# A Mamba-2 mixer inside a two-layer decoder trunk: grouping the small TensorE products of the scan

## The chip, the cores and the metric

The kernel runs on one core of a Trainium2 chip. Time is device time in microseconds; the kernel before took 1373.68 us, the median of three runs (1373.65 to 1373.69). One more execution was taken with the hardware profiler. A core has five engines with a queue each: TensorE (PE in the profile; its weight loads are PEld), VectorE (DVE), ScalarE (ACT), GpSimd (POOL) and SyncE (SP, which here only issues DMAs). Each engine takes its instructions in the order of its queue, and engines wait for each other by semaphores.

## The reference

The reference is a trunk of two layers on x of shape (1, 512, 1024), all float32: a Mamba-2 mixer, a convolutional FFN, shared keys and values, differential attention and a second FFN. The change lies in the mixer alone, whose core is this:

```python
def ssd_chunked(xdt, a, bm, cm):
    ...
    a_cs = jnp.cumsum(ac, axis=-1)
    decay_in = jnp.exp(segsum(ac))
    cb = jnp.einsum('bclgn,bcsgn->bcgls', cc, bc)
    y_diag = jnp.einsum('bcgls,bgrcls,bcsgrp->bclgrp', cb, decay_in, xc)
    decay_states = jnp.exp(a_cs[..., -1:] - a_cs)
    states = jnp.einsum('bclgn,bgrcl,bclgrp->bcgrpn', bc, decay_states, xc)
    ...
    y_off = jnp.einsum('bclgn,bcgrpn,bgrcl->bclgrp', cc, states_in, jnp.exp(a_cs))
    return (y_diag + y_off).reshape(b, s, h, p)

def mamba2_mixer(x, ln_g, in_w, conv_w, conv_b, dt_bias, a_log, d_skip, norm_g, out_w):
    zxbcdt = rms_norm(x, ln_g) @ in_w
    ...
    xbc = jax.nn.silu(causal_dwconv(xbc, conv_w, conv_b))
    ...
    y = ssd_chunked(xs32 * dt[..., None], a, bm.astype(jnp.float32), cm.astype(jnp.float32))
    y = y + xs32 * d_skip.astype(jnp.float32)[:, None]
    y = y.reshape(b, s, D_INNER) * jax.nn.silu(z.astype(jnp.float32))
    y = rms_norm(y.reshape(b, s, SSM_GROUPS, D_INNER // SSM_GROUPS), ...)
    return y @ out_w
```

There are 4 groups of 8 heads of 64 columns, 4 chunks of 128 tokens, and 128 states. A chunk's output has a part from the chunk itself (C B^T, times the decays, times x) and a part from the state that the chunks before it left.

## The kernel before, in words

**Projections.** Activations lie transposed: features on the 128 partitions, 512 tokens along the free dimension. A column block of 128 features of the input projection is 24 TensorE products of 128 x 512: for each of 8 row blocks, `mm3` multiplies high weights with high activations (L190), high with low (L191) and low with high (L192). The high and low parts are fp32r numbers, split from float32: the weights' high part by ScalarE (L141), the low part by VectorE (L145). `chunk` makes these splits two blocks ahead. Raw weights come by DMA on SP's queue into three buffers.

**A group.** The loop over g (0 to 3) fetches the decays of its four chunks (POOL's queue: `m`, L609, 512 KB each, and `er`, L614), then projects and convolves B (`bT`), C (`cT`) and four x blocks (`xs`) in `conv_block`. Then comes the scan, woven with the four z blocks. After it VectorE multiplies xs by the activated z (L761, here called gating), ScalarE squares it (L763, `gsq`), POOL and VectorE sum the squares (L768, `gacc`), TensorE transposes the sum (L441, `tr_g`), VectorE takes the inverse root, and TensorE spreads it over the tokens (L451, `al_g`). Group 0's norm stands in the stream of group 1's projections; the other groups have the output projection of the group before in between.

**A chunk of the scan.** `tokens` transposes x (four transposes, L639, `xs` in PSUM), multiplies by dt (`xd`, L641) and by the decay to the chunk's end (`xe`, L644), and transposes B (L646, `bt`), which ScalarE copies (L648). `masked` computes C B^T (L630, `cb`) and multiplies it into the decays `m` (L631), on which `decays` has run POOL's causal mask (L619) and eight ScalarE exponentials (L624) before. `states` computes the part from the state before (L656, `yo`; times `er`, L658) and the new state (L661, `st`; copied by ScalarE for chunk 0, L664, updated by VectorE for others, L666 and L667). `outputs` computes the chunk's own part (L676, `y`) and adds it to x (L680, L683). Transposes are one pass each; the float32 products are two.

**What sets the order.** The source traces instructions, and a list scheduler of the framework sets each engine's order by their dependences and its own estimates. Three things steer it: the order in which the source traces them; `pin`, which keeps an instruction in the traced order; and `tc.issue_after(i)`, which puts what is traced inside it behind instruction i on that instruction's engine. `weave(main, fill, num, den)` traces num steps of `fill` for every den of `main`. PSUM has eight banks of 128 x 512 float32: four for the wide products (`mm_bank`) and four for all else (`aux_bank`).

Of the kernel before, what the change touches and what calls it, by code (L numbers as in the profile page):

```python
# [2 lines left out]

# [1 line left out]

# [4 lines left out]
F32 = mybir.dt.float32  # L10
# [8 lines left out]
P = 128  # L19
T = 512  # L20
D = 1024
KB = D // P
# [17 lines left out]
def trunk_kernel(ctx: ExitStack, tc, x, ssm_ln_g, ssm_in_w, ssm_conv_w, ssm_conv_b, ssm_dt_bias,  # L40
# [19 lines left out]
    def aux_bank(name):  # L60
        return pp.tile([P, T], F32, tag="aux", name=name)
# [127 lines left out]
    def mm3(ps, wh, wl, xh, xl, start, stop):  # L189
        pe.matmul(ps, wh, xh, start=start, stop=False)  # L190
        pe.matmul(ps, wh, xl, start=False, stop=False)  # L191
        pe.matmul(ps, wl, xh, start=False, stop=stop)  # L192


    ones = cp.tile([P, P], F32, name="ones")
# [307 lines left out]
    with tc.tile_pool(name="ssm_y", bufs=1) as yp, tc.tile_pool(name="ssm", bufs=1) as sp:  # L503
        def in_block(key):
            wh, wl = chunk(key)
            if key in ("in32", "in36"):
                return ps_b0 if key == "in32" else ps_b1
            ps = mm_bank("ps_" + key)
            for k in range(KB):
                mm3(ps, wh[:, k, :], wl[:, k, :], xgh[k], xgl[k], k == 0, k == KB - 1)  # L510
            return ps

        def conv_block(j, key, dst):
            ps = in_block(key)
# [78 lines left out]
        class Chunk:  # L593


            def __init__(self, g, c, bT, cT, xs, prev):
                self.g, self.c, self.bT, self.cT, self.xs, self.prev = g, c, bT, cT, xs, prev
                self.hh = slice(c * NH + g * HPG, c * NH + (g + 1) * HPG)
                self.cs = slice(c * P, (c + 1) * P)
                self.tag = "%d_%d" % (g, c)  # L600

            def per_head(self, cols):
                return cols[:, self.hh].unsqueeze(2).to_broadcast([P, HPG, 64])
# [21 lines left out]

            def masked(self):

                cs = self.cs
                ps = aux_bank("cb" + self.tag)
                pe.matmul(ps[:, :P], self.bT[:, cs], self.cT[:, cs], start=True, stop=True)  # L630
                dve.tensor_tensor(out=self.m, in0=self.m, in1=ps[:, :P].unsqueeze(1).to_broadcast([P, HPG, P]),  # L631
                                  op=ALU.mult)

            def tokens(self):

                tag, cs = self.tag, self.cs
                ps = aux_bank("xs" + tag)
                for b in range(4):
                    pe.transpose(ps[:, b * P:(b + 1) * P], self.xs[:, b, cs], ident)  # L639
                self.xd = sp.tile([P, HPG, 64], F32, tag="xd", name="xd" + tag, bufs=2)  # L640
                dve.tensor_tensor(out=self.xd, in0=byh(ps), in1=self.per_head(dt), op=ALU.mult)  # L641
                if self.c < NT - 1:
                    self.xe = sp.tile([P, HPG, 64], F32, tag="xe", name="xe" + tag, bufs=2)
                    dve.tensor_tensor(out=self.xe, in0=self.xd, in1=self.per_head(dl), op=ALU.mult)  # L644
                    ps = aux_bank("bt" + tag)
                    pe.transpose(ps[:, :P], self.bT[:, cs], ident)  # L646
                    self.bt = sp.tile([P, P], F32, tag="bt", name="bt" + tag, bufs=2)
                    act.activation(self.bt, ps[:, :P], AF.Copy)  # L648

            def states(self):  # L650
# [43 lines left out]
                    add_to_stream(m, ps, 16, norm)  # L694
                    yield

        def z_blocks(g, zs):
            for b in range(4):
                ps = in_block("in%d" % (4 * g + b))
                z = sp.tile([P, T], F32, tag="z", name="z%d_%d" % (g, b), bufs=4)  # L700
                dve.tensor_tensor(out=z, in0=ps, in1=rr[0], op=ALU.mult)
                act.activation(z, z, AF.Silu)
                zs.append(z)
                yield
# [36 lines left out]
        for g in range(NG):  # L741
            bT = sp.tile([P, T], F32, tag="bT", name="bT%d" % g, bufs=2)
            cT = sp.tile([P, T], F32, tag="cT", name="cT%d" % g, bufs=2)
            xs_ = sp.tile([P, 4, T], F32, tag="xs", name="xs%d" % g, bufs=2)
            cs = chunks(g, bT, cT, xs_)
            for c in cs:
                c.fetch()
            conv_block(16 + g, "in%d" % (32 + g), bT)
            conv_block(20 + g, "in%d" % (36 + g), cT)
            if g == 0:  # L750
                params_a()
            xs = [xs_[:, b, :] for b in range(4)]
            for b in range(4):
                if b >= 2:
                    cs[b - 2].decays()
                conv_block(4 * g + b, "in%d" % (16 + 4 * g + b), xs[b])
            zs = []
            weave(scan(cs), z_blocks(g, zs), 2, 3)
            acc = None
            for b in range(4):  # L760
                dve.tensor_tensor(out=xs[b], in0=xs[b], in1=zs[b], op=ALU.mult)  # L761
                sq = sp.tile([P, T], F32, tag="gsq", name="gsq%d_%d" % (g, b), bufs=2)
                act.activation(sq, xs[b], AF.Square)  # L763
                if b == 0:
                    acc = sq
                else:
                    a2 = sp.tile([P, T], F32, tag="gacc", name="gacc%d_%d" % (g, b), bufs=2)
                    (pool if b == 1 else dve).tensor_tensor(out=a2, in0=acc, in1=sq, op=ALU.add)  # L768
                    acc = a2
            if g == 0:  # L770
                params_b()
                prev = normed(g, xs, acc)
            elif g < NG - 1:
                run(out_proj(g - 1, *prev, None))
                prev = normed(g, xs, acc)
            else:
                op = out_proj(g - 1, *prev, None)
                for _ in range(3):
                    next(op)
                prev = normed(g, xs, acc)  # L780
                run(op)
# [322 lines left out]
```

## Time and profile before

| What | Value |
|---|---|
| median of 3 runs | 1373.68 us (1373.65 to 1373.69) |
| the profiled execution, own time | 1374.65 us |
| its span (first to last instruction) | 1373.0 us |
| PE busy | 1357.5 us, 99% |
| DVE busy | 917.2 us, 67% |
| ACT busy | 666.0 us, 49% |
| granted TensorE clock | 0.999 |

All times of the trace count from the span's start. A row of the timeline gives start and length in us, engine, source line, operation, output tile <- inputs, sizes and a count; in square brackets the engine's idle time before it and who ended it. Ends of matmuls are modelled, and matmuls overlap, so the distance from one start to the next tells more than a length. A row of the view of waits gives the waiter, whom it waited for, the sum in us, how often, and the longest.

### The profile page before, as it was taken

How to read it: one execution, taken by the hardware profiler on the slowest of the kernel's cores; microseconds unless marked ns; L12 is line 12 of the kernel's file. 1: busy time of each engine (PE TensorE's matmuls, PEld its weight loads, DVE VectorE, ACT ScalarE, POOL GpSimd, SP SyncE). 2: the span in 40 equal slices, each digit the busy share in tenths (PEclk: the TensorE clock that was granted, in tenths of full speed). 3: DMA queues.
4: the chain of work that ended last, by engine and by line, in shares of the span. 5: the costliest groups of instructions: out<-in, count | busy, mean ns of one | idle time of the engine just before them, and what ended most of it. 6: DMA issues, size and time to landing. Idle time of an engine off the chain costs nothing.

```text
span 1373.0 us, 16922 instructions
## 1 busy us (share of the span) xinstructions
PE 1357.5 (99%) x6421; PEld 1097.7 (80%) x6421; DVE 917.2 (67%) x1527; ACT 666.0 (49%) x1100; POOL 94.1 (7%) x121
## 2 busy tenths in 40 slices
PE   9999999999999999999999999999999999999998
PEld 7877887887878888888888877776778888888886
DVE  5989788688877774367755456757787773367741
ACT  5696745552444442244434457758554442244431
POOL 4230301100110000000002000000110000000000
PEclk9999999999999999999999999999999999999999
DMA  7542433432233323333323322221223333333231
GB/s 200 153 151 81 146 105 106 136 89 70 92 92 104 96 92 101 99 93 96 96 87 108 116 77 77 63 81 47 61 87 104 92 96 104 93 93 106 85 104 58
DMA packets 187618, 135.07 MB, mean 98 GB/s; under 512 B 6540, under 2 KB 176976, under 8 KB 187536
## 3 DMA queue, kind: packets, MB, share of 16 engines
q1 hardware_dynamic: 180736, 120.84, 29.2%
q0 software_dynamic: 4496, 12.05, 2.8%
q10 hardware_dynamic: 2304, 1.10, 0.3%
q8 instruction: 50, 0.82, 0.2%
q14 instruction: 32, 0.26, 0.1%
HBM read 131.72 MB, written 2.25 MB: 98 GB/s over the span
## 4 chain that ended last, share of the span: by engine, by line
PE 87%; DVE 7%; ACT 4%; issue 1%; DMA 0%; POOL 0%; POOLq 0%; SPq 0%; ACTq 0%
PE ps_d L192 6%; PE ps_d L190 6%; PE ps_d L191 6%; PE ps_u L190 6%; PE ps_u L192 6%; PE ps_u L191 6%; PE ps_g L191 6%; PE ps_g L192 6%; PE ps_g L190 6%; PE ps_in L191 4%; PE ps_in L190 4%; PE ps_in L192 4%; PE ps_o L191 2%; PE ps_o L192 2%; PE ps_o L190 2%
## 5 line engine op out<-in xcount | busy, mean ns | idle before, releaser
L191 PE MATMUL ps_g<-xgl,wh_g 128*128 128x512 f32 x352 | 137.3, 390 | 1.6 <-DVE xgl L409 1.6
L190 PE MATMUL ps_d<-hh,wh_d 128*128 128x512 f32 x352 | 137.6, 391 | 0.0
L190 PE MATMUL ps_u<-xgh,wh_u 128*128 128x512 f32 x352 | 137.4, 390 | 0.0
L192 PE MATMUL ps_d<-hh,wl_d 128*128 128x512 f32 x352 | 137.4, 390 | 0.0
L190 PE MATMUL ps_g<-xgh,wh_g 128*128 128x512 f32 x352 | 137.2, 390 | 0.0
L191 PE MATMUL ps_d<-hl,wh_d 128*128 128x512 f32 x352 | 137.1, 390 | 0.0
L192 PE MATMUL ps_u<-xgh,wl_u 128*128 128x512 f32 x352 | 137.1, 390 | 0.0
L191 PE MATMUL ps_u<-xgl,wh_u 128*128 128x512 f32 x352 | 137.1, 389 | 0.0
L192 PE MATMUL ps_g<-xgh,wl_g 128*128 128x512 f32 x352 | 137.1, 389 | 0.0
L190 PE MATMUL ps_in<-xgh,wh_in 128*128 128x512 f32 x304 | 121.0, 398 | 0.0
L191 PE MATMUL ps_in<-xgl,wh_in 128*128 128x512 f32 x304 | 120.9, 398 | 0.0
L192 PE MATMUL ps_in<-xgh,wl_in 128*128 128x512 f32 x304 | 119.7, 394 | 0.0
L145 DVE TENSOR_TENSOR wl_d<-wr_d,wh_d 128x1024 fp32r<-128x1024 f32 (+1 forms) x48 | 54.5, 1135 | 91.8 <-ACT wh_d L141 91.6
L141 ACT ACTIVATE wh_d<-wr_d 128x1024 fp32r<-128x1024 f32 (+1 forms) x48 | 47.5, 990 | 129.2 <-PE ps_d L191 115.3
L818 ACT ACTIVATE hh<-vg 128x512 fp32r<-128x512 f32 x44 | 27.8, 632 | 114.9 <-DVE vg L817 114.9
L801 DVE TENSOR_TENSOR uu<-ps_u,nr_f 128x512 f32<-128x512 f32 x44 | 30.4, 692 | 77.6 <-PE ps_u L192 77.5
L191 PEld LDWEIGHTS ps_g<-xgl,wh_g 128*128 128x128 f32 x352 | 66.1, 188 | 15.9 <-DVE xgl L409 2.3
L190 PEld LDWEIGHTS ps_g<-xgh,wh_g 128*128 128x128 f32 x352 | 66.1, 188 | 14.0 <-ACT xgh L408 0.5
L192 PEld LDWEIGHTS ps_u<-xgh,wl_u 128*128 128x128 f32 x352 | 66.1, 188 | 13.8
L192 PEld LDWEIGHTS ps_g<-xgh,wl_g 128*128 128x128 f32 x352 | 66.1, 188 | 13.7
L192 PEld LDWEIGHTS ps_d<-hh,wl_d 128*128 128x128 f32 x352 | 66.1, 188 | 13.7
L191 PEld LDWEIGHTS ps_d<-hl,wh_d 128*128 128x128 f32 x352 | 66.1, 188 | 13.6
(340 smaller groups left out, 2980.4 us busy)
## 6 DMA issues: line engine op xcount, KB each, us to landing
wr_g<-in_ffn_up_w_dram SPq DMA_DIRECT2D x44, 512.0 KB, 3.7
wr_u<-in_ffn_up_w_dram SPq DMA_DIRECT2D x44, 512.0 KB, 3.7
wr_in<-in_ssm_in_w_dram SPq DMA_DIRECT2D x40, 512.0 KB, 3.8
wr_d<-in_ffn_down_w_dram SPq DMA_DIRECT2D x40, 512.0 KB, 3.3
m<-cumd POOLq DMA_DIRECT2D x16, 512.0 KB, 4.6
wr_out<-in_ssm_out_w_dram SPq DMA_DIRECT2D x16, 512.0 KB, 3.5
wr_k<-in_kv_w_dram SPq DMA_DIRECT2D x8, 512.0 KB, 3.7
wr_q<-in_q_w_dram SPq DMA_DIRECT2D x8, 512.0 KB, 3.7
```

What stands on the lines that cost most here:

```text
L141: return act.activation(self.wh[:, :self.n], self.raw[:, :self.n], AF.Copy)
L145: return dve.tensor_tensor(out=self.wl[:, :self.n], in0=self.raw[:, :self.n], in1=self.wh[:, :self.n].bitcast(F32), op=ALU.subtract)
L190: pe.matmul(ps, wh, xh, start=start, stop=False)
L191: pe.matmul(ps, wh, xl, start=False, stop=False)
L192: pe.matmul(ps, wl, xh, start=False, stop=stop)
L801: dve.tensor_tensor(out=u, in0=ps, in1=r, op=ALU.mult)
L818: act.activation(h, ga, AF.Copy)
```

## The change

C B^T and the B transpose leave `masked` and `tokens` for a new method `keys`. For chunks 0 and 1 of a group it is traced behind the second x block, with `issue_after` the block's last product; for chunks 2 and 3 right behind `tokens`, as part of the scan. z blocks 0 and 1 are traced ahead of the scan, and the x transposes of chunks 0 and 1 are put, with `issue_after`, behind the product of row block 5 (of 0 to 7) of z block 1. The weave of the scan with the two remaining z blocks takes 2 steps in 5, in place of 2 in 3.

```diff
@@ mm3, in_block
-        pe.matmul(ps, wl, xh, start=False, stop=stop)
+        return pe.matmul(ps, wl, xh, start=False, stop=stop).ins
...
-                mm3(ps, wh[:, k, :], wl[:, k, :], xgh[k], xgl[k], k == 0, k == KB - 1)
+                state["last"] = mm3(ps, wh[:, k, :], wl[:, k, :], xgh[k], xgl[k], k == 0, k == KB - 1)
+                if k == 5:
+                    state["late"] = state["last"]
@@ Chunk
+                self.place = nullcontext
...
             def masked(self):
-                cs = self.cs
-                ps = aux_bank("cb" + self.tag)
-                pe.matmul(ps[:, :P], self.bT[:, cs], self.cT[:, cs], start=True, stop=True)
+                ps = self.cb
...
             def tokens(self):
-                for b in range(4):
-                    pe.transpose(ps[:, b * P:(b + 1) * P], self.xs[:, b, cs], ident)
+                with self.place():
+                    for b in range(4):
+                        pe.transpose(ps[:, b * P:(b + 1) * P], self.xs[:, b, cs], ident)
...
-                    ps = aux_bank("bt" + tag)
-                    pe.transpose(ps[:, :P], self.bT[:, cs], ident)
-                    self.bt = sp.tile([P, P], F32, tag="bt", name="bt" + tag, bufs=2)
+
+            def keys(self):
+                cs = self.cs
+                self.cb = aux_bank("cb" + self.tag)
+                with self.place():
+                    pe.matmul(self.cb[:, :P], self.bT[:, cs], self.cT[:, cs], start=True, stop=True)
+                if self.c < NT - 1:
+                    ps = aux_bank("bt" + self.tag)
+                    with self.place():
+                        pe.transpose(ps[:, :P], self.bT[:, self.cs], ident)
+                    self.bt = sp.tile([P, P], F32, tag="bt", name="bt" + self.tag, bufs=2)
                     act.activation(self.bt, ps[:, :P], AF.Copy)
@@ z_blocks, scan, the loop over groups
+                if b == 1:
+                    for c in cs[:2]:
+                        c.place = partial(tc.issue_after, state["late"])
...
                     cs[t].tokens()
+                    if t > 1:
+                        cs[t].keys()
                     cs[t].masked()
...
                 conv_block(4 * g + b, "in%d" % (16 + 4 * g + b), xs[b])
+                if b == 1:
+                    for c in cs[:2]:
+                        c.place = partial(tc.issue_after, state["last"])
+                        c.keys()
...
-            weave(scan(cs), z_blocks(g, zs), 2, 3)
+            zb = z_blocks(g, zs, cs)
+            next(zb)
+            next(zb)
+            weave(scan(cs), zb, 2, 5)
```

More of the change, by code (lines that the diff above doesn't have):

```diff
@@ L1 @@
 import math
-from contextlib import ExitStack
+from contextlib import ExitStack, nullcontext
+from functools import partial
 import numpy as np
@@ L695, in out_proj, with z_blocks @@
                     yield
-        def z_blocks(g, zs):
+        def z_blocks(g, zs, cs):
             for b in range(4):
                 ps = in_block("in%d" % (4 * g + b))
+                if b == 1:
+                    for c in cs[:2]:
+                        c.place = partial(tc.issue_after, state["late"])
                 z = sp.tile([P, T], F32, tag="z", name="z%d_%d" % (g, b), bufs=4)
```

## The prediction

> **What bounds the kernel now.** I read the page first: busy shares and the chain that ended last.
>
> ```profile
> span 1373.0 us, 16922 instructions
> PE 1357.5 (99%) x6421; PEld 1097.7 (80%) x6421; DVE 917.2 (67%) x1527; ACT 666.0 (49%) x1100; POOL 94.1 (7%) x121
> ...
> PE 87%; DVE 7%; ACT 4%; issue 1%; DMA 0%; POOL 0%; POOLq 0%; SPq 0%; ACTq 0%
> ```
>
> TensorE is busy for 1357.5 of 1373.0 us and carries 87% of the chain. The change can therefore save only what TensorE loses between its products, and can cost only what makes TensorE wait. Next I took the busy times of a stage, the scan of group 1, and TensorE's waits from the first scan to the last.
>
> ```profile
> core 0: us, PE busy (x) PEld busy (x) DVE busy (x) ACT busy (x) POOL busy (x), PEclk, DMA share, GB/s
> 121.50:149.00 27.50, 27.50 (x169) 20.95 (x167) 26.29 (x44) 15.25 (x27) 5.27 (x7) 1.00 0.36 119
> ...
> PE al_g L451 <- DVE tr_g L424: 0.6, 2, 0.3
> PE tr_g L441 <- DVE gacc L768: 0.5, 1, 0.5
> PE st L661 <- DVE xe L644: 0.2, 1, 0.2
> ```
>
> In this scan TensorE has no idle time at all and its full clock (1.00), but VectorE comes next: 26.29 of 27.50 us. The waits that TensorE shows there sum to 1.3 us. So little is to be won, and the danger is VectorE's queue.
>
> **What the change does to the order.** All instructions stay: the same transposes, the same C B^T products, the same copies. What changes is how often TensorE leaves its 512-wide products for a small run of other instructions; call such a run a visit. Counted in the order of the built programs, group 0 goes from 15 visits to 11, group 1 from 12 to 6 (one of its new ones joins the broadcast of the norm), groups 2 and 3 from 8 to 6 each: 14 fewer. In groups 1 to 3 the eight x transposes land behind the whole second z block and not behind a part of it. The C B^T and B transposes land behind the second x block.
>
> **Term 1, the visits.** A visit's price comes from the timeline of group 1 (start, length, engine, line, operation, output<-inputs, count), where two visits hold nothing but two transposes each.
>
> ```profile
> 126.39 0.39 PE L190 MATMUL ps_in<-xgh,wh_in 128*128 128x512 f32 x1
> ...
> 128.43 0.39 PE L190 MATMUL ps_in<-xgh,wh_in 128*128 128x512 f32 x1
> 128.66 0.38 PE L639 MATMUL xs<-ident,xs 128*128 128x128 f32 x2
> 128.79 0.48 PE L191 MATMUL ps_in<-xgl,wh_in 128*128 128x512 f32 x1
> ...
> 131.18 0.38 PE L639 MATMUL xs<-ident,xs 128*128 128x128 f32 x2
> 131.31 0.48 PE L192 MATMUL ps_in<-xgh,wl_in 128*128 128x512 f32 x1
> ...
> 133.70 1.02 PE L661 MATMUL st<-xe,bt 128*128 128x512 f32 x2
> ```
>
> From 126.39 to 128.43 are nine steps: 2.04 / 9 = 0.227 us a product. From 131.18 to 133.70 are ten products and two transposes: 2.52 - 2.27 = 0.25 us for the pair, of which the transposes themselves are 0.38 - 0.27 = 0.11 us each (a lone one lasts 0.27, the row of bt below). So a visit costs 0.25 - 0.22 = 0.03 to 0.04 us of switching. 14 x 0.04 = 0.56 us saved. That the 14 are worth more is bounded by the dearest visit below.
>
> **Term 2, short waits inside visits.** The B transpose and C B^T of the second chunk wait for a bank that is not yet emptied; the last two rows are from the view of waits and show whom the weight loader waited for (sum, times, longest).
>
> ```profile
> 121.79 0.27 PE L646 MATMUL bt<-ident,bT 128*128 128x128 f32 x1
> ...
> 123.27 0.39 PE L191 MATMUL ps_in<-xgl,wh_in 128*128 128x512 f32 x1
> 123.52 0.33 PE L646 MATMUL bt<-ident,bT 128*128 128x128 f32 x1
> 123.60 0.47 PE L192 MATMUL ps_in<-xgh,wl_in 128*128 128x512 f32 x1
> 123.92 0.39 PE L190 MATMUL ps_in<-xgh,wh_in 128*128 128x512 f32 x1
> 124.22 0.49 PE L630 MATMUL cb<-cT,bT 128*128 128x128 f32 x2
> 124.46 0.48 PE L191 MATMUL ps_in<-xgl,wh_in 128*128 128x512 f32 x1
> 124.78 0.40 PE L192 MATMUL ps_in<-xgh,wl_in 128*128 128x512 f32 x1
> ...
> PEld cb L630 <- ACT bt L648: 0.9, 3, 0.3
> PEld bt L646 <- ACT bt L648: 0.6, 3, 0.3
> ```
>
> From 123.92 to 124.78 stand two products (0.45) and two passes (0.22): 0.19 us over, 0.15 of it waiting. The bt visit, 123.27 to 123.92, is 0.65 - 0.45 - 0.11 = 0.09 over, 0.05 waiting. That is 0.2 us a group in three groups, the same three in which the weight loader waited (0.9 + 0.6 us there is the upper bound, most of it hidden behind running products). Once issued together behind a product-filled x block, these instructions find banks free. I take 0.6 us saved, between 0.3 and 1.5.
>
> **Term 3, the tail of group 0.** Two things move here. z blocks 0 and 1 now precede the scan, so the last y visit stands four products later in the stream (4 x 0.227 = 0.9 us); and VectorE splits one weight chunk behind that visit which it used to split before it. Group 0's norm then waits for `gacc`, as it did already.
>
> ```profile
> 89.40 0.68 DVE L701 TENSOR_TENSOR z<-ps_in,nr_x 128x512 f32<-128x512 f32 x1
> ...
> 90.60 1.22 DVE L145 TENSOR_TENSOR wl_in<-wr_in,wh_in 128x1024 fp32r<-128x1024 f32 x1
> 91.74 1.89 DVE L761 TENSOR_TENSOR xs<-xs,z 128x512 f32<-128x512 f32 x3
> ...
> 91.85 1.28 ACT L702 ACT_TABLE_LOAD   x1
> 93.14 0.63 ACT L702 ACTIVATE z<-z 128x512 f32<-128x512 f32 x1
> ...
> 94.63 1.13 ACT L763 ACTIVATE gsq<-xs 128x512 f32<-128x512 f32 x2
> ...
> 95.82 1.21 DVE L145 TENSOR_TENSOR wl_in<-wr_in,wh_in 128x1024 fp32r<-128x1024 f32 x1
> 95.85 2.33 POOL L768 TENSOR_TENSOR gacc<-gsq,gsq 128x512 f32<-128x512 f32 x1 [1.10 <-ACT gsq L763]
> ...
> 98.87 0.69 DVE L768 TENSOR_TENSOR gacc<-gacc,gsq 128x512 f32<-128x512 f32 x1 [1.85 <-ACT gsq L763]
> ...
> 100.08 0.68 DVE L768 TENSOR_TENSOR gacc<-gacc,gsq 128x512 f32<-128x512 f32 x1
> ...
> 164.62 1.29 POOL L768 TENSOR_TENSOR gacc<-gsq,gsq 128x512 f32<-128x512 f32 x1 [2.51 <-ACT gsq L763]
> ```
>
> Later by 0.9 (position) and 1.1 (one more split, 91.74 - 90.60). Earlier by 0.6 (the z evacuation at 89.40, which leaves the tail) and by about 1.4 on ScalarE: the first gating ends near 92.4 and its square could follow, but starts at 94.63, because a table load and the activation of z stand before it, which now come earlier. Of those 2.2 us the split of a weight, which stays, keeps some 0.9. Between the last two sums (98.87 and 100.08, 1.2 apart) the changed order puts a convolution step that waits for its ScalarE half, itself behind the last square (1.13 for two): I estimate 0.6 more. Together 0.9 + 1.1 - 0.6 - 1.4 + 0.6 = 0.6, less about 0.1 for the visits before it: +0.5 us of wait, if POOL's sum is lengthened again. Bounds: -0.5 (the whole old wait goes) to +2.3.
>
> [...]
>
> **Terms at nothing, with their cover.** Group 0's first state copy on ScalarE now queues behind all 32 exponentials and a table load; the second chunk's yo products need it.
>
> ```profile
> 68.56 9.48 ACT L624 ACTIVATE m<-m,ncum 128x128 f32<-128x128 f32 x32
> ...
> 132.69 1.29 DVE L644 TENSOR_TENSOR xe<-xd,dec 128x512 f32<-128x512 f32 x2
> ...
> 61.96 2.02 DVE L644 TENSOR_TENSOR xe<-xd,dec 128x512 f32<-128x512 f32 x2
> ```
>
> Let T be the start of the eight x transposes. z's activation ends about T + 1.5, a table load takes about 1.3, so the copy comes at T + 2.8 + 9.5 + 0.6 = T + 12.9. The yo products stand 49 products (11.1 us) plus the x, st, y and B visits (about 3.8) after T: T + 14.9. The cover is 2.0 us; if it were gone, yo would wait for the rest.
>
> The st product behind the x transposes is closer. VectorE runs z's evacuation (0.6), xd, xd, xe in that order: T + 0.25 + 4 x 0.6 + 0.1 = T + 2.75, and 0.2 to reach TensorE. TensorE comes there at T + 8 x 0.11 + 9 x 0.227 + 0.1 = T + 3.0. I take 0, with 0.1 us to spare; bounds -0.2 (the wait of today goes) and +0.64 a group (xe took 2.02 for 1.29 once, 0.74 more). Bank waits of the parameter transposes in group 0 and of the last B transpose in group 1 have no row; the nearest are 0 and the 0.3 of a bt wait. I take 0.2 for both. SP's queue keeps its order. The split that moves into the tail stood 4 us earlier, so it frees its raw buffer some 4 us later, and the transfer that waits for that buffer starts later too:
>
> ```profile
> wr_in<-in_ssm_in_w_dram SPq DMA_DIRECT2D x40, 512.0 KB, 3.8
> ```
>
> At 3.8 us it still lands before its own split, which comes three weight chunks further on, 24 products or 5.4 us each. POOL's queue swaps fetches and masks of the next group, due blocks later.
>
> **Sum.** -0.56 - 0.6 + 0.5 + 0.2 = -0.46 us. The profiled execution took 1374.65 us around its span of 1373.0, 0.97 above the median of 1373.68; so 1374.2 for a profiled one and 1373.2 for the median. 0.2%, 2.75 us, is about what a measurement of this kernel tells from no change; this lies well inside.
>
> **Rivals.** (a) st waits for xe in all four groups. Place: st, nine products behind the transposes. For it: only 0.1 us to spare, and the 0.2 us wait that is there today. Against: in the changed order nothing but z's evacuation stands before xd. It decides from the first VectorE instruction of over 0.1 us that gets in front; at a split's 1.14 us, four groups cost 4 x 1.04 = 4.2 us: 1373.2 + 4.2 = 1377.4. Chance 0.07.
> (b) The tail of group 0 collides more: a mask of POOL against the gating, a split against POOL's sum, about 1 us each. For it: 2.33 us above. Against: one such collision is in the old time already. 1373.2 + 1.8 = 1375.0. Chance 0.13.
> (c) Visits are worth more than 0.04: if each of the 14 cost the 0.19 of the C B^T visit above, 2.7 us go and no more is lost in the tail: 1371.0. For it: group 1's row. Against: most of that 0.19 was waiting, and the pure pair shows 0.04. Chance 0.1.
> (d) It does nothing: group 0 gives back all that groups 1 to 3 save: 1373.7. Chance 0.2. The order did change, so the saving exists; only its size and group 0's loss are open.
> The forecast, 1372.4 to 1373.6, has the remaining 0.5.
>
> **How the numbers follow.** The range takes in the forecast, (b) and (d), and goes down towards (c): 1371.6 to 1375.2. Faster by over 0.2% (below 1370.9) holds half of (c) and a little: 0.06. Slower by over 0.2% (above 1376.4) holds (a) and a little of (b): 0.08. Within: 0.86.
>
> **What would show it.** Right: the scans of groups 2 and 3 come 0.3 to 0.5 us shorter, with st free of a wait and no bt or cb row over 0.3 us; tr_g in group 0 waits about 1 us for gacc instead of 0.5. Wrong: a wait at st <- xe in several groups (a); tr_g waiting 2 us or more (b); scans shorter by over 0.6 us each (c); a wait at yo <- S in group 0, which would undo the cover of 2.0 us.

## The result and the profile after

| | before | after |
|---|---|---|
| median, both measured side by side | 1373.48 us (1372.65 to 1374.26, 22 executions) | 1375.62 us (1374.04 to 1378.93, 22 executions) |
| ratio of the medians | | 1.0016, 95% interval 1.0010 to 1.0021 |
| profiled execution, own time | 1374.65 us | 1376.37 us |
| its span | 1373.0 us | 1374.5 us |

The change costs 2.1 us, 0.16%. The forecast was 1373.2 us with a range up to 1375.2. First the page of the kernel after, its busy times and the chain that ended last, and TensorE's waits in the mixer:

```profile
PE 1357.7 (99%) x6421; PEld 1098.5 (80%) x6421; DVE 918.6 (67%) x1527; ACT 657.0 (48%) x1092; POOL 96.7 (7%) x121
...
PE 86%; DVE 7%; ACT 4%; issue 2%; DMA 0%; POOL 0%; SPq 0%; ACTq 0%; POOLq 0%; DVEq 0%
```

```profile
PE tr_g L442 <- DVE s2t L394: 2.2, 1, 2.2
PE al_g L452 <- DVE tr_g L425: 1.6, 3, 1.0
PE st L673 <- DVE xe L647: 0.3, 1, 0.3
```

The shares tell nothing. The waits do: tr_g in group 0 waits 2.2 us instead of 0.5, and al_g 1.6 us instead of 0.6, 1.0 of them in one place (group 3). To see where the time went, take the starts of the same TensorE products in both kernels: the first product of group 0's, group 1's and group 2's output projection, the first feed-forward product, and ScalarE's last copy of the output. Before:

```profile
157.12 0.39 PE L190 MATMUL ps_o<-yh,wh_out 128*128 128x512 f32 x1
...
248.43 0.39 PE L190 MATMUL ps_o<-yh,wh_out 128*128 128x512 f32 x1
...
339.73 0.39 PE L190 MATMUL ps_o<-yh,wh_out 128*128 128x512 f32 x1
...
384.40 0.39 PE L190 MATMUL ps_g<-xgh,wh_g 128*128 128x512 f32 x1
...
1368.59 0.38 ACT L846 ACTIVATE o<-ot 128x256 f32<-128x256 f32 x1 [0.53 <-PE ot L845]
```

After:

```profile
160.50 0.39 PE L191 MATMUL ps_o<-yh,wh_out 128*128 128x512 f32 x1
...
251.54 0.39 PE L191 MATMUL ps_o<-yh,wh_out 128*128 128x512 f32 x1
...
342.59 0.39 PE L191 MATMUL ps_o<-yh,wh_out 128*128 128x512 f32 x1
...
388.27 0.39 PE L191 MATMUL ps_g<-xgh,wh_g 128*128 128x512 f32 x1
...
1371.15 0.38 ACT L870 ACTIVATE o<-ot 128x256 f32<-128x256 f32 x1 [0.53 <-PE ot L869]
```

| stretch (differences of these starts) | before | after | change |
|---|---|---|---|
| start to the first output projection (groups 0 and 1) | 157.12 | 160.50 | +3.38 |
| period of group 2 | 91.31 | 91.04 | -0.27 |
| period of group 3 | 91.30 | 91.05 | -0.25 |
| last two output projections | 44.67 | 45.68 | +1.01 |
| feed-forward and attention, to the last copy | 984.19 | 982.88 | -1.31 |
| last copy to the span's end (1373.0, 1374.5) | 4.4 | 3.4 | -1.0 |

So groups 2 and 3 gain what the prediction saw in them, and the loss sits in two places of the mixer: group 0 with its tail, and the wait of 1.0 us at al_g in group 3. The last two rows lie in code that the change does not touch; the last experiments are about them.

**The tail of group 0.** The timeline of the kernel after, VectorE, GpSimd and ScalarE, with the instructions that decide:

```profile
88.60 0.69 DVE L670 TENSOR_TENSOR er<-yo,er 128x512 f32<-128x512 f32 x1 [1.00 <-PE yo L668]
...
91.73 1.28 POOL L623 TENSOR_SCALAR_AFFINE_SELECT m<-m 128x1024 f32<-128x1024 f32 x1
91.97 1.58 DVE L695 TENSOR_TENSOR xs<-xs,er 128x512 f32<-128x512 f32 x1
93.48 1.21 DVE L146 TENSOR_TENSOR wl_in<-wr_in,wh_in 128x1024 fp32r<-128x1024 f32 x1
94.61 3.75 DVE L785 TENSOR_TENSOR xs<-xs,z 128x512 f32<-128x512 f32 x4
94.90 1.10 POOL L623 TENSOR_SCALAR_AFFINE_SELECT m<-m 128x1024 f32<-128x1024 f32 x1
...
96.59 1.23 ACT L787 ACTIVATE gsq<-xs 128x512 f32<-128x512 f32 x2 [1.30 <-DVE xs L785]
...
97.91 1.60 POOL L792 TENSOR_TENSOR gacc<-gsq,gsq 128x512 f32<-128x512 f32 x1 [1.91 <-ACT gsq L787]
...
102.11 0.68 DVE L792 TENSOR_TENSOR gacc<-gacc,gsq 128x512 f32<-128x512 f32 x1
```

Read it against the rows of the prediction. The gating starts at 94.61 instead of 91.74, 2.87 us later. ScalarE's first squares start at 96.59 instead of 94.63: ScalarE now waits for VectorE (1.30), where before it was ScalarE's own queue that was late. The last sum comes at 102.11 instead of 100.08. Two masks of GpSimd run beside VectorE, and each time VectorE's row is longer: 1.58 us for a product that takes 0.68 elsewhere, 3.75 for four gatings that take 2.50 where no mask disturbs them (a row of the next section). What follows on TensorE:

```profile
100.34 0.39 PE L193 MATMUL ps_in<-xgh,wl_in 128*128 128x512 f32 x1
102.94 0.63 PE L442 MATMUL tr_g<-ident,gacc 128*128 128x128 f32 x4 [2.21 <-DVE s2t L394]
103.32 0.66 PE L191 MATMUL ps_in<-xgh,wh_in 128*128 128x512 f32 x1
...
106.76 0.45 PE L193 MATMUL ps_in<-xgh,wl_in 128*128 128x512 f32 x1
107.05 0.39 PE L191 MATMUL ps_in<-xgh,wh_in 128*128 128x512 f32 x1
```

Behind the stand-still the products start (106.76 - 103.32) / 8 = 0.43 us apart instead of 0.227 (PEclk of that stretch: 0.52), and then at full speed again. From 103.32 to 107.05 are nine steps in 3.73 us, 1.69 more than 9 x 0.227. The windows over group 0's tail confirm it by the granted clock (PEclk, third number from the end), before and then after:

```profile
94.60:121.50 26.90, 26.36 (x121) 21.46 (x120) 24.59 (x50) 22.04 (x36) 2.48 (x2) 1.00 0.27 74
```

```profile
94.60:121.50 26.90, 24.69 (x110) 19.97 (x109) 25.35 (x50) 19.13 (x37) 3.00 (x3) 0.94 0.48 126
```

0.06 x 26.9 = 1.6 us of clock were lost. So this execution lost 1.7 us of waiting (2.2 - 0.5) and again 1.7 us of clock.

### The profile page after: what moved, and what is told of

It reads as the page before. It is cut to its first block, busy times and chain, and to the rows that moved or that the text cites. A ratio compares the mean times of both kernels' runs of the same rounds, so it can differ in the third digit from the quotient of the medians.

```text
span 1374.5 us, 16913 instructions
## 1 busy us (share of the span) xinstructions
PE 1357.7 (99%) x6421; PEld 1098.5 (80%) x6421; DVE 918.6 (67%) x1527; ACT 657.0 (48%) x1092; POOL 96.7 (7%) x121
## 4 chain that ended last, share of the span: by engine, by line
PE 86%; DVE 7%; ACT 4%; issue 2%; DMA 0%; POOL 0%; SPq 0%; ACTq 0%; POOLq 0%; DVEq 0%
PE ps_d L193 6%; PE ps_d L191 6%; PE ps_d L192 6%; PE ps_g L191 6%; PE ps_g L193 6%; PE ps_g L192 6%; PE ps_u L191 6%; PE ps_u L193 6%; PE ps_u L192 6%; PE ps_in L191 4%; PE ps_in L192 4%; PE ps_in L193 4%; PE ps_o L193 2%; PE ps_o L192 2%; PE ps_o L191 2%
## 5 line engine op out<-in xcount | busy, mean ns | idle before, releaser
L192 PEld LDWEIGHTS ps_u<-xgl,wh_u 128*128 128x128 f32 x352 | 66.2, 188 | 13.5
L191 PEld LDWEIGHTS ps_u<-xgh,wh_u 128*128 128x128 f32 x352 | 66.1, 188 | 13.6
```

## The experiments

Each section gives the edit, what was expected, what came out and what follows. Lines that begin with + or - are against the kernel named.

### The change in groups 1 to 3 alone, and in group 0 alone

Every new step is made dependent on the group; the other groups keep the order of before.

```diff
+            if g > 0:            # second kernel: g == 0
                 next(zb)
                 next(zb)
-            weave(scan(cs), zb, 2, 5)
+            weave(scan(cs), zb, 2, 5 if g > 0 else 3)
```

> The change in groups 1 to 3 only; group 0 keeps the old order of transposes, C B^T and z blocks. Theory (the loss is all in the tail of group 0, a longer wait of tr_g for gacc and a halved TensorE clock behind it): these three groups gained 0.26 us each between their output projections, so 0.8 us faster than before, 1372.7, tr_g in group 0 waits 0.5 us as before, no stretch at half clock. Rival (grouping costs in every group, through st waiting for xe or VectorE's queue): slower than before, 1374 to 1375.

> The change in group 0 only. Theory: all of the loss is here, so 2.1 + 0.8 = 2.9 us slower than before, 1376.4 at the median, with single times spread over more than 2 us, because the clock halves in some runs and not in others; tr_g waits about 2.2 us. Rival (the loss comes from all groups alike): a quarter of 2.1 us, 1374.0, with a spread under 1 us.

Groups 1 to 3 alone: 1372.65 us (1371.98 to 1373.32, 11 executions), ratio 0.9993 (0.9984 to 1.0002). Group 0 alone: 1377.38 us (1375.68 to 1378.23, 9), ratio 1.0026 (1.0016 to 1.0035). The loss is group 0's: groups 1 to 3 alone come out neither slower nor, by an interval that reaches over 1, surely faster. With the change in groups 1 to 3 alone, al_g of group 3 still waits 1.0 us:

```profile
PE al_g L452 <- DVE tr_g L425: 1.6, 3, 1.0
```

With group 0 alone tr_g waits 3.6 us, more than in the whole change and than the 2.2 expected, and the timeline shows why: here GpSimd, not VectorE, is the one that is held up.

```profile
90.99 5.43 POOL L623 TENSOR_SCALAR_AFFINE_SELECT m<-m 128x1024 f32<-128x1024 f32 x1
...
92.97 2.50 DVE L792 TENSOR_TENSOR xs<-xs,z 128x512 f32<-128x512 f32 x4
...
96.45 1.28 ACT L628 ACTIVATE m<-m,ncum 128x128 f32<-128x128 f32 x4 [3.09 <-POOL m L623]
...
98.86 1.28 POOL L799 TENSOR_TENSOR gacc<-gsq,gsq 128x512 f32<-128x512 f32 x1 [0.34 <-ACT gsq L794]
...
100.84 0.69 DVE L799 TENSOR_TENSOR gacc<-gacc,gsq 128x512 f32<-128x512 f32 x1 [3.35 <-ACT gsq L794]
```

The mask that takes 1.10 us elsewhere took 5.43, the four gatings their undisturbed 2.50. On ScalarE the exponentials of that mask, which stand ahead of the squares, wait 3.09 us for it. That wait shows the lateness without the span on GpSimd, which is rough. So the squares are late; GpSimd's sum waits for them and comes at 98.86, and VectorE then waits 3.35 us for the squares behind that sum. Whoever loses the meeting, the chain to tr_g is late: by the gating in the kernel after (3.75 us for 2.50), by the mask here (5.43 for 1.10). Why a row is longer beside the other engine's, and which of the two it will be, was not shown.

### The norm of group 0 issued later

The whole change, with group 0's norm put behind the first x block of group 1; and the same with the change in groups 1 to 3 only.

```diff
-                prev = normed(g, xs, acc)
+                held = (g, xs, acc)
...
+                if g == 1 and b == 0:
+                    with tc.issue_after(state["last"]):
+                        prev = normed(*held)
```

> The whole change, with group 0's norm (tr_g and all that follows) issued 15 products later, behind group 1's x block 0. Theory: TensorE no longer stands still for gacc, so the wait of 2.2 us and the half clock both go: 1372.4 (1374.3, the runs at full clock, less the 2.2 us wait, plus 0.3 for what moves), and the spread shrinks to that of before. Rival (the wait is only a sign of VectorE being too late, and comes back at al_g or at the next scan): 1374 or more, with a wait of 1 us or more at al_g, cb or st.

> The change in groups 1 to 3 only, and group 0's norm 15 products later. Theory: the 0.8 us of the three groups and the 0.5 to 0.7 us that TensorE waited for gacc before: 1372.0 to 1372.2, faster than both kernels. Rival (the wait comes back at al_g): 1372.7, the same as the change in groups 1 to 3 alone.

1378.17 us (1377.54 to 1379.03, 6 executions), ratio 1.0031 (1.0019 to 1.0044); with groups 1 to 3 only 1372.82 us (1372.60 to 1373.26, 11). My theory fell in both: the wait at tr_g is gone, but it comes back at al_g, in the whole change larger than it was.

```profile
PE al_g L452 <- DVE tr_g L425: 5.0, 4, 3.3
...
106.00:125.00 19.00, 15.65 (x63) 12.72 (x62) 16.91 (x36) 13.15 (x20) 0.00 (x0) 0.82 0.31 85
```

The second line is the window behind it: PEclk 0.82, so 0.18 x 19 = 3.4 us of clock lost; if the clock was halved there as in the kernel after, that is about 6.8 us of it, an estimate. Where TensorE meets the chain is not the matter; the chain on VectorE is late. Why it comes later still here, I only read from the order: VectorE has the next blocks' convolutions between the steps of the inverse root.

### A longer stand-still in the kernel before

The first products of group 1's x block 0 are issued behind tr_g, in the kernel before and without anything of the change; nine products in the first kernel, six in the second.

```diff
+                with tc.issue_after(state["turned"]) if key == "in21" or key == "in20" and k >= 0 else nullcontext():
-                mm3(ps, wh[:, k, :], wl[:, k, :], xgh[k], xgl[k], k == 0, k == KB - 1)
+                    mm3(ps, wh[:, k, :], wl[:, k, :], xgh[k], xgl[k], k == 0, k == KB - 1)
```

> The kernel before, with one thing moved: the nine products of group 1's x block 0 that stand ahead of group 0's transposes tr_g, and the block behind it, are issued behind tr_g, so that tr_g is met at product 304 instead of 313 and TensorE has 9 x 0.227 = 2.0 us less to do while VectorE's gating and sums run. Nothing else of the change is in it. Theory (a stand-still of TensorE of about two microseconds is by itself followed by a stretch at half clock, whatever caused it): tr_g waits 0.5 + 2.0 = 2.5 us, a stretch of 3.4 us at granted clock 0.5 follows as in the kernel after, and the time is 1373.5 + 2.0 + 1.7 = 1377.2 us, or up to 0.9 more if the second wait, al_g, has less in front of it. Rival (the half clock of the kernel after comes from something else in the change): the same wait, the clock stays at 1.0, 1375.5 us (to 1376.4).

> As the run with tr_g at product 304, with six products moved instead of nine: tr_g is met at product 307, so it waits 0.5 + 6 x 0.227 = 1.9 us. It asks where between 1.0 us (the al_g wait of the run with the change in groups 1 to 3 alone, clock 1.0) and 2.2 us (the kernel after, clock 0.5) the clock begins to fall. Theory of a threshold at about two microseconds: 1.4 us more than before with the clock at 1.0, 1374.9 us; if the half clock comes already here, 1376.6 us.

Nine products: 1375.12 us (1374.59 to 1376.96, 10 executions), ratio 1.0015 (1.0006 to 1.0025). Six: 1373.92 us (1373.16 to 1374.77, 10), ratio 1.0002 (0.9993 to 1.0011). The waits are 2.1 and 1.4 us, 0.4 to 0.5 shorter than I had reckoned. By the median the nine products came out as the rival had it (1375.5, not 1377.2). The six were to cost 1.4 us and cost 0.3: their first output projection does start 1.29 us later than before (158.41 for 157.12), but their program's end takes 3.4 us instead of 4.4, of which the last runs tell. In the profile with 2.1 us the products behind it run at full speed:

```profile
100.95 0.65 PE L441 MATMUL tr_g<-ident,gacc 128*128 128x128 f32 x4 [2.07 <-DVE gacc L769]
...
101.68 0.39 PE L191 MATMUL ps_in<-xgl,wh_in 128*128 128x512 f32 x1
101.91 0.40 PE L192 MATMUL ps_in<-xgh,wl_in 128*128 128x512 f32 x1
```

The kernel after had half clock behind 2.2 us. So about the same wait is followed by half clock in some executions and not in others. What tells it apart without a profile is the mean granted clock of an execution: 3.4 us at half clock take 1.7 us / 1374 = 0.0012 off it, and the profiles with such a stretch have a mean of 0.998 or less, those without one 0.999 or more. Counted are executions at 0.998 or less. The stand-still is that of the profiled execution; how long the others stood still is not on record:

| stand-still in group 0 | kernel | at 0.998 or less |
|---|---|---|
| 0.5 | before, measured beside these runs | 0 of 84 |
| 1.4 | six products moved; masks moved (next section) | 0 of 10, 0 of 11 |
| 2.1 | nine products moved | 2 of 10 |
| 2.2 | the kernel after, twice | 7 of 22, 5 of 10 |
| 3.3 | norm later | 5 of 6 |
| 3.6 | change in group 0 alone; without the moved keys | 7 of 9, 5 of 10 |

Of the two kernels with 3.6 us one profile shows the stretch and the other, after the same wait, the full clock. By this count a stand-still of 2.1 us brings a lower clock in some executions without anything else of the change. That rests on two executions (1376.32 and 1376.24 us, 1.2 above their median), and the one profile of that kernel does not show the stretch itself. Up to 1.4 us no execution fell to 0.998; from 2.1 us on a part of them did.

### GpSimd's masks out of the tail

The whole change; the masks of group 1's chunks 2 and 3 behind GpSimd's sum.

```diff
+                with tc.issue_after(state["summed"]) if self.g == 1 and self.c >= 2 else nullcontext():
-                pool.affine_select(out=self.m, in_=self.m, ...)
+                    pool.affine_select(out=self.m, in_=self.m, ...)
```

> The whole change, with GpSimd's masks of group 1's chunks 2 and 3 issued behind its sum in group 0's tail, so that none runs beside VectorE's gating. Theory (the masks stretch the gating row from 2.5 to 3.75 us and the row before it from 0.68 to 1.58 us, 2.1 us in all, and this is what made tr_g wait 2.2 us instead of about 0.5): the gating takes 2.5 us, tr_g waits under 0.8 us, no half clock, 1375.6 - 1.7 - 1.7 = 1372.2 us. Rival (VectorE is late for another reason: the scan's last products of group 0 stand at TensorE's products 257 to 268 instead of 248 to 265, while tr_g stays at product 313): the rows become shorter but tr_g waits more than 1.5 us, and the time stays within 0.7 us of the kernel after, 1374.9 to 1376.3 us.

1374.06 us (1373.50 to 1374.69, 11 executions), ratio 1.0003 (0.9994 to 1.0012). Both expectations missed, between them: the gating is undisturbed and 1.2 us earlier, but tr_g still waits 1.4 us.

```profile
93.40 2.49 DVE L786 TENSOR_TENSOR xs<-xs,z 128x512 f32<-128x512 f32 x4
...
94.11 1.24 ACT L788 ACTIVATE gsq<-xs 128x512 f32<-128x512 f32 x2 [0.31 <-DVE xs L786]
...
97.00 3.57 POOL L624 TENSOR_SCALAR_AFFINE_SELECT m<-m 128x1024 f32<-128x1024 f32 x2
98.05 1.57 DVE L793 TENSOR_TENSOR gacc<-gacc,gsq 128x512 f32<-128x512 f32 x1
...
99.54 1.57 DVE L524 SCALAR_TENSOR_TENSOR ctmp<-u,c,ctmp 128x511 f32<-128x511 f32 x1
...
101.03 0.68 DVE L793 TENSOR_TENSOR gacc<-gacc,gsq 128x512 f32<-128x512 f32 x1
```

The moved masks now run beside the sums: a sum takes 1.57 us instead of 0.68, and the convolution step between the last two sums 1.57 instead of 0.75, 1.7 us together. So this run exchanges one meeting for another and does not tell what the order costs by itself. Taking these masks off the gating is worth 0.8 us of the wait (2.2 to 1.4); what is left, 1.4, is no more than the 1.7 of the new meeting.

### One z block ahead in group 0, and the keys left in place there

First, the whole change, but only one z block is traced ahead of group 0's scan. Second, both z blocks ahead, but C B^T and B's transposes of group 0 stay chunk by chunk.

```diff
             next(zb)
-            next(zb)
+            if g > 0:
+                next(zb)
```

> The whole change, but in group 0 one z block ahead of the scan instead of two, so that two z blocks are left behind the scan's last step as in the kernel before: yo of chunks 1 to 3 stand at products 246, 248 and 262 (before 248, 249 and 263; after 257, 257 and 267), tr_g at 312. Keys and C B^T stay moved together. Theory of the order (the second z block ahead of the scan takes 4 to 9 products, 0.9 to 2.0 us, from the work that stands behind the scan's end, and VectorE's tail is late by that): tr_g waits at most 1.0 us, clock 1.0 throughout, 1372.3 to 1373.0 us, as with the change in groups 1 to 3 alone. Rival (keys and the changed issue of group 0, not the z block, make the tail late): the tr_g wait stays at 2 us, with the half clock, 1375 to 1376.5 us.

> The whole change, but in group 0 C B^T and B's transposes stay chunk by chunk; the two z blocks ahead of the scan stay. The scan's last products stand at 257 to 267 as in the kernel after. Theory (the z blocks alone make the tail late): tr_g waits 2 to 3.6 us, a stretch at half clock in most executions, 1374.3 to 1377.4 us. Rival (it takes the moved keys as well): tr_g waits under 1 us, clock 1.0, about 1372.7 us.

One z block: 1372.73 us (1371.85 to 1373.36, 11 executions), ratio 0.9995 (0.9986 to 1.0003). Keys left in place: 1377.20 us (1374.80 to 1378.77, 10), ratio 1.0020 (1.0011 to 1.0030). The waits of tr_g in the first and the second:

```profile
PE tr_g L442 <- DVE s2t L394: 0.3, 1, 0.3
```

```profile
PE tr_g L442 <- DVE s2t L394: 3.6, 1, 3.6
```

Both theories held, but for the half clock, which came in 5 of 10 executions and not in most. The second z block ahead of the scan is what makes the tail late: without it the wait is gone, and with it, even with the keys left in place, it is there. With it the scan's last visits stand 4 to 9 products nearer to tr_g. These runs don't part the lateness from the masks that it meets: with one z block the gating takes 2.51 us, undisturbed, and with the keys left in place it is again the mask that is held up, for 5.42 us.

### Each half of the change by itself

First, only C B^T and B's transposes moved, in all groups; second, only the z blocks and x transposes, in groups 1 to 3.

```diff
                     for c in cs[:2]:
                         c.place = partial(tc.issue_after, state["last"])
                         c.keys()
+                        c.place = nullcontext
...
-            next(zb)
-            next(zb)
-            weave(scan(cs), zb, 2, 5)
+            weave(scan(cs), zb, 2, 3)
```

> Only half of the change, in all four groups: C B^T and B's transposes of the first two chunks together behind the second x block; z blocks and x transposes as before. Groups 2 and 3 have 9 visits in the 336 products of a group's period, before 10, after 8. The period takes 91.31 us before and 91.05 after. Theory of visits and bank waits as the prediction priced them (0.04 for a visit, 0.2 of bank waits, all with the keys): 91.31 - 0.24 = 91.1 us here. Rival (the gain sits in the x transposes and the z blocks): 91.25 us or more. Group 0's tail keeps its order, so tr_g waits at most 0.7 us at full clock. Time 1372.4 to 1373.6 us.

> The other half, in groups 1 to 3 alone: two z blocks ahead of the scan and the x transposes together behind the second; C B^T and B's transposes stay where they were, chunk by chunk. Group 0 is as before. 9 visits a period. Theory (the gain comes with the keys): the period stays above 91.2 us. Rival: 91.1 us or less. al_g of group 3 tells which half brings the new wait of 1.0 us: if it is the z blocks (VectorE's work of the scan ends 19 products nearer to the norm), it waits 1.0 us here and 0.3 or less in the run with the keys alone.

Keys alone: 1372.96 us (1372.10 to 1374.67, 10 executions), ratio 0.9994 (0.9985 to 1.0003). z blocks and x transposes alone: 1373.51 us (1372.68 to 1374.57, 10), ratio 0.9998 (0.9989 to 1.0007). The periods of group 2, worked out as in the table above, are 91.49 and 91.19 us, beside 91.31 before and 91.04 after. My theory fell: the keys alone make a period longer, and the other half, at 91.19, lies between theory and rival. The timeline of the keys alone shows what they bring:

```profile
218.48 0.39 PE L191 MATMUL ps_in<-xgh,wh_in 128*128 128x512 f32 x1
219.01 0.44 PE L642 MATMUL xs<-ident,xs 128*128 128x128 f32 x2
```

The last x transposes come 0.53 us behind the product before them, where 0.23 is the step: without the keys beside them they are issued earlier, and wait for ScalarE's convolution of x block 3. Less that 0.3 us, each half would save 0.12. Only the two halves together save 0.27: the keys leave the scan, and the x transposes stand late enough to wait for nothing. al_g of group 3 waits no longer than 0.3 us in either half, but that does not settle which half brings the 1.0 us. With the z blocks and x transposes alone, 25 products and not 17 stand between tr_g and al_g of group 3:

```profile
348.12 0.63 PE L442 MATMUL tr_g<-ident,gacc 128*128 128x128 f32 x4 [0.20 <-DVE gacc L795]
...
354.45 0.62 PE L452 MATMUL al_g<-ident,tr_g 128*128 128x128 f32 x4
```

This order hides a late inverse root, and tr_g itself waits there: the last two output projections take 45.05 us instead of 44.67. With the keys alone, over 17 products, they take 44.67. So this half already has some of the loss; whether it has all of it stays open.

### al_g of group 3 eight products later

The kernel with one z block ahead in group 0; in group 3 al_g goes behind the fifth of eight output blocks.

```diff
-            r = along_tokens(token_rsqrt(acc, sp, "g%d" % g, 512), "g%d" % g)
+            r = token_rsqrt(acc, sp, "g%d" % g, 512)
+            if between:
+                between()
+            with tc.issue_after(state["product"]) if between else nullcontext():
+                r = along_tokens(r, "g%d" % g)
```

> The run with one z block ahead of group 0's scan, and in group 3 the transposes al_g moved eight products (1.8 us) further back in the out-projection of group 2. In that run al_g of group 3 waits 1.0 us for VectorE's inverse root, and the stretch of 192 products from the first of group 2's out-projection takes 45.67 us instead of before's 44.67. Theory (this new wait is a loss of its own in the kernel after too, and nothing behind al_g is that urgent): the stretch falls back to 44.7 us and the time to 1372.7 - 1.0 = 1371.7 us. Rival (the first products of group 3's own out-projection come to wait instead): the stretch stays at 45.5 to 45.9 us, 1372.7 us.

1371.85 us (1371.29 to 1373.04, 11 executions), ratio 0.9986 (0.9976 to 0.9995). As the theory had it, the wait is gone, and the last two output projections take 383.62 - 339.15 = 44.5 us:

```profile
339.15 0.39 PE L191 MATMUL ps_o<-yh,wh_out 128*128 128x512 f32 x1
...
383.62 0.39 PE L191 MATMUL ps_g<-xgh,wh_g 128*128 128x512 f32 x1
```

This is the one version whose interval lies below the kernel before. 1.0 us of its distance is again the end of the program, of which the last runs tell.

### Second profiles

The kernel before, the kernel after, and the change in groups 1 to 3 alone, each unchanged, profiled once more. The question was what the last two rows of the table above are.

> The kernel before, profiled a second time. Its first profile took 1374.65 us, 1.0 above its median, and has a stand-still of 1.0 us ahead of the first feed-forward products (waiting for xgl) that no other kernel's profile has. Theory (an accident of that execution: VectorE and GpSimd meet in another phase): this profile lacks it, the waits of groups 0 to 3 are the same (tr_g 0.5, al_g 0.3), and the median is 1373.6 us again. Rival (it belongs to the kernel, and the other kernels gain 1 us there): the wait is back at 1.0 us.

> The kernel after, profiled a second time. Theory: the tr_g wait is 2.0 to 2.4 us again (its cause is the order, the same in every execution), while the half clock may be there or not; without it the profile's own time is about 1374.3 us and its span 1372.7 us. From the last ScalarE copy to the end of the span: 3.4 us if this belongs to the build, 4.4 us or anything between if it belongs to the execution.

> The change in groups 1 to 3 alone, profiled a second time. From the last ScalarE copy to the end of the span 3.4 us again if it belongs to the build; then 1.0 us of its distance to the kernel before is not the change's, and its rows (0.7 us less in the groups, 1.0 us more at al_g of group 3) leave about 0.3 us of loss. If it is 4.4 us here, the end varies by execution, and the median of 1372.65 us stands for the change. al_g of group 3 waits 1.0 us in either case.

Before: 1373.87 us (1373.16 to 1375.57, 10 executions). After: 1377.22 us (1374.22 to 1380.44, 10), ratio 1.0020 (1.0010 to 1.0031). Groups 1 to 3: 1373.16 us (1372.39 to 1373.35, 10), ratio 0.9992 (0.9982 to 1.0001). The kernel after came out 1.6 us above its first measurement, 3.2 above the kernel before beside it; more of its executions fell to 0.998 (5 of 10, against 7 of 22). In its profile tr_g waits 2.2 us again, this time at full clock (PEclk 1.00 in the window 94.60 to 121.50). Its first output projection starts at 158.81, 1.69 us earlier than in the first profile: that is the price of the half clock alone. But the first feed-forward products have a wait of their own, 1.0 us of this row:

```profile
PE ps_g L192 <- DVE xgl L410: 1.5, 2, 1.0
```

The first profile of before had it too, the second had 0.5 in all:

```profile
PE ps_g L191 <- DVE xgl L409: 1.6, 2, 1.0
```

So the -1.31 in the table is an accident of an execution that comes in either kernel. One expectation missed: the second profile of before has no wait of 0.5 us at tr_g.

```profile
100.53 0.66 PE L441 MATMUL tr_g<-ident,gacc 128*128 128x128 f32 x4
```

It starts 0.50 us behind the product ahead of it, where in the first profile it was 0.92. In the first profile a mask stood beside the last gating, and GpSimd's sum behind them took 2.33 us; in the second it took 1.90. So the old wait too is not the same in every execution. The end is not such an accident: from the last copy to the span's end it takes 4.4 us in both profiles of before and 3.4 in both of after and both of the third kernel. That microsecond belongs to the build. What in a build sets it is open: all other builds showed 3.4 us, but for 3.7 with the z blocks and x transposes alone and 3.8 with nine products moved.

## Why the prediction was wrong

**Terms 1 and 2 held in their sum.** Visits and bank waits were priced at 0.08 + 0.2 us for groups 2 and 3 each; the table shows 0.27 and 0.25. How the sum divides is not confirmed: by the prices the keys alone bring 0.24 and the other half 0.04, and the halves show 0.12 each, the keys' only after their new wait of 0.3 is taken off.

**Term 3 is the step that failed: the +0.5 us of wait, made of 0.9 + 1.1 - 0.6 - 1.4 + 0.6 - 0.1; 1.7 came.** Of GpSimd it took in only the sum; the masks it put at nothing ("due blocks later") and left to rival (b). Follow the chain. The row of VectorE that waits for the last yo starts at 88.60; before it was this one:

```profile
87.33 0.69 DVE L658 TENSOR_TENSOR er<-yo,er 128x512 f32<-128x512 f32 x1
```

That is 1.27 us later, where position was priced at 0.9. The split and the removed z evacuation came as priced. The product of xs with er took 0.90 us more beside a mask (1.58 for 0.68). So the gating was 2.87 us late, not 0.9 + 1.1 - 0.6 = 1.4. The credit on ScalarE was there: with the masks moved away the squares start 0.71 us behind the gating's start (94.11 and 93.40), where before it was 2.89. But in the kernel after a mask stands beside the gating itself, the squares start 1.98 us behind it, and 0.9 of the 1.4 us is left. GpSimd's sum was not lengthened as much again (1.60 us, before 2.33), and the convolution step between the sums cost 0.7, near its 0.6. In all the last sum comes 2.03 us later, and the two meetings with masks are about 2.1 of what made it late (0.90, and 1.98 - 0.71 = 1.27).

So the way of rival (b) is what happened, brought on by the order: the second z block ahead of the scan is shown to be needed by the run with one z block (0.3 us of wait). That the masks carry the loss, and not the lateness by itself, is worked out from rows; no run has the new order without such a meeting. The 1.7 us lies inside the bounds that the term itself gave (-0.5 to +2.3).

**Two terms were missing.** The first is the clock. I had priced a stand-still at its own length. Behind 2.2 us the clock was halved for about 3.4 us in one profile of two, 1.7 us more, and by the mean clock in part of the other executions. The second is al_g of group 3, 1.0 us: I looked for late VectorE work in the tail of group 0, where a wait stood already, and not in the tails of the other groups, where the yo and y visits also moved towards the norm. In both kernels its cover is the 17 products between tr_g and al_g, and the run with eight more products of cover (44.5 us against 45.7) shows that nothing else holds it.

**The sum after the fact,** from rows: -0.8 for groups 1 to 3 (0.2 to 0.3 for group 1: from group 0's tr_g to the first output projection it is 56.30 us before, 56.13 with the change in groups 1 to 3 alone, 55.98 in the second profile of after), +1.0 for al_g, +1.7 for tr_g, +0.6 for the clock (1.7 us in 12 of 32 executions), -1.0 for the end that belongs to the build: +1.5 us, beside +2.1 measured first and +3.2 the second time. What is missing is open. In the second profile of before tr_g stood 0.42 us closer behind its product, so an execution of before without that wait would hold part of it.

**The rivals.** (b) was priced at 1375.0, with about 1 us for a meeting from the rows before (GpSimd's sum 2.33 us beside a split of VectorE, 1.29 at 164.62); the measured 1375.6 lies above it and above the range, for neither the clock nor al_g was in its price. (a), st waiting for xe, was 0.3 us once instead of 0.2: nothing. It is not out of reach: with the keys alone it was 0.7 us in group 0, and 0.8 in the run with al_g later. (c) would have shown scans over 0.6 us shorter; they are 0.27. (d) let group 0 give back what groups 1 to 3 save; their 0.8 us is already given back by al_g's 1.0 in group 3. The 0.8 to 1.0 us by which the run with groups 1 to 3 lies under the kernel before is therefore not the saving of the scan; the end is 1.0 us shorter.

## What to carry to other kernels

When small work is collected and put earlier, ask what it used to stand next to: the products that it displaces may have been the cover of another engine's serial chain, and that chain has to be followed to its end in every stage, not only where a wait is visible today. Ask as well which work of a third engine the moved chain now runs beside. Price a credit on one engine only after checking that the engine which feeds it is not late itself. A stand-still of TensorE of 2.2 us cost nearly twice its length in the first profile of the kernel after (2.2 us of wait and 1.7 of clock), and the clock fell in 12 of the 32 executions measured, so it is worth breaking up or covering before shorter ones.

## What the runs showed of the hardware that was not expected

- **The clock fell after short stand-stills, and not in every execution.** Counted by the mean clock, and with the wait of the profiled execution: never after 1.4 us (0 of 21 executions), in 2 of 10 after 2.1 us, in 12 of 32 after 2.2 us, in 12 of 19 after 3.6 us; the slow stretch lasts about 3.4 us (103.32 to 106.76 in the first profile of after, PEclk 0.52). The stand-still ahead of it was 2.2 us, or 2.6 us (100.73 to 103.32) if the four transposes of tr_g are counted into the gap. In the second profile of after the same 2.2 us was followed by full clock (1.00), and without the moved keys so was 3.6 us. What decides it was not shown.
- **Either side can lose a meeting of VectorE and GpSimd.** A mask of 1.10 us took 5.43 beside a row of VectorE instructions in one kernel, and in another the mask kept its 1.10 while VectorE's gating went from 2.50 to 3.75 us.
- **The end of the program differs by 1.0 us between builds** that have the same instructions there (4.4 and 3.4 us from the last copy to the span's end), more than the whole saving of the scan. Two kernels that differ by a microsecond should be compared by the starts of the same products, and not by their times alone.
